# A fp32 decoder layer on one core: where the first norm takes its gain from, who adds the weight sums, and the order of attention's transposes

## The chip, the cores and the metric

The kernel runs on one core of one Trainium2 chip. The metric is the device time of one execution in microseconds (us), the median of several executions. TensorE (PE) multiplies matrices, its weight loads (PEld) run beside it, VectorE (DVE), ScalarE (ACT) and GpSimd (POOL) work element by element, and SyncE (SP) issues the DMAs.

## What is computed

One decoder layer in fp32 with three residual steps, for 16 meta tokens and 1024 tokens of width 1024: a half-step SwiGLU (d_ff 2816), a mix of eight stick-breaking attention heads and eight RWKV-7 heads, and a second half-step SwiGLU; then a last norm without the meta tokens. Cut to the core (the heads' inner functions are left out):

```python
h = jnp.concatenate([meta, x], axis=1)
for l in range(DEPTH):
    n = rms_norm(h, ffn1_norm[l])
    h = h + 0.5 * swiglu(n, ffn1_w_gate[l], ffn1_w_up[l], ffn1_w_down[l])
    n = rms_norm(h, mix_norm[l])
    proj = n @ w_in[l]
    q, k, v = ...                      # 8 heads of 64
    sb_out = stick_breaking_attention(q, k, v)
    rw_out = rwkv7_time_mix(proj[..., 3 * SB_WIDTH:], ...)
    h = h + jnp.concatenate([sb_out, rw_out], axis=-1) @ w_out[l]
    n = rms_norm(h, ffn2_norm[l])
    h = h + 0.5 * swiglu(n, ffn2_w_gate[l], ffn2_w_up[l], ffn2_w_down[l])
return rms_norm(h, final_norm)[:, N_META:]
# A[t,s] = sigmoid(z_ts) * prod_{s<j<t} (1 - sigmoid(z_tj)), o_t = sum_{s<t} A[t,s] v_s
```

## The kernel before

**Arithmetic.** Every fp32 operand is split in two: `split` (L473) lets ACT copy it to a rounded high part and DVE (or POOL, where it is told so) subtract that from the source for the low part. `mm3` (L638) then issues three matmuls for one product: high by high, low by high, high by low. A weight tile arrives by an SP DMA in `wraw` (two buffers), and `wsplit` (L501) makes `whi` (ACT) and `wlo` (DVE) of it.

**Stages.** The tokens go in two groups, A with 528 and B with 512. TensorE's order is FFN1 of A (0 to some 400 us), the projections and part of RWKV of A, FFN1 of B (from 586 us) with RWKV units and A's attention (918 to 1049) strewn in, projections of B, w_out of A, FFN2 of A (from 1323) with RWKV and attention of B (1555 to 1782), w_out of B, FFN2 of B (the last part from 2020 to 2245 in quads) and the last norm.

**Order.** A planner (class `Clock`) runs the kernel's generators as tasks with priorities, holds its own costs for each operation, and emits the one whose data and buffers (`need`) are due; what it emits is the order on each engine. So a moved operation can reorder its neighbours.

**Start.** `xfirst` (L2092) spreads the first norm's gain over the partitions by two matmuls (tile `pg1` in the code, `pg` in the trace), DVE copies them to `g1b`; `block` (L816) multiplies the two first token blocks by `g1b`, scales them by the root (`xn`), transposes them (`pxn`) and splits them to `nh`, `nl`. `raw` (L2128) transposes the raw tokens (`px`) for the residual `h`.

**Quads.** For d_ff tiles from 6 on in FFN1 of A, and at the end of FFN2 of B, gate and up products of two tiles are made with seven half products instead of eight. `pair` (L550) makes the weight sums s1 to s4 (tiles `qs`) on POOL and splits each to `qh`, `ql`; the `quad` generator (L1071) multiplies. There are 30 such pairs. `ups2` (L924) splits the result to `ah` (ACT) and `al` (POOL).

**FFN1 of B.** `ffn` (L851) has `mm`, `gate`, `up`, `down`. The first two d_ff tiles are made for tokens 0 to 256 and then for 256 to 512, and their weights are loaded and split anew for each. `load_n1` (L2308) fetches the normed tokens of B (`nh`, `nl` from the scratch tensor `nbd`) on SP. Beside it, RWKV's `prep` makes the tiles `x` on DVE, for the products `pG`.

**Attention.** `attn_av` (L1815): `trs` transposes one group of weights (`pat`) of the first head, then of the second; the value products (`po`) of the group before follow once its splits (`ath`, `atl`) are done.

**End.** `final_last` (L1992) transposes the last scaled rows (`po`), then adds up the sums of squares (`fss`, twelve and four passes) for the root `fst`; DVE and ACT scale the output `ot`, SP stores it.

Every instruction goes through one recorder, so all rows name line L101: the tiles tell them apart.

Of the kernel before, what the change touches and what calls it, by code (L numbers as in the profile page):

```python
# [16 lines left out]
P = 128  # L17
# [434 lines left out]
class Ker:  # L452
# [48 lines left out]
    def wsplit(self, raw, nk, nm, pool):  # L501
        self.clock.ahead = True
        hi = pool.tile([P, nk, nm], F32R, tag="wh", bufs=2, name="whi")
        lo = pool.tile([P, nk, nm], F32R, tag="wl", bufs=2, name="wlo")
        self.split(hi, lo, raw)
        self.clock.ahead = False
        return hi, lo
# [42 lines left out]
    def pair(self, raws, out):  # L550
# [7 lines left out]
        def part(src=None):  # L558
# [8 lines left out]
            if src:  # L567
                x, y, op = src
                raw = p.tile([P, 4, P], F32, tag="qs", bufs=3, name="qs")
                self.hold((raw,))  # L570
                nc.gpsimd.tensor_tensor(out=raw, in0=x, in1=y, op=op)
# [16 lines left out]
        s1 = yield from part((a2[:, lo4], a2[:, hi4], ALU.add))  # L588
# [5 lines left out]
        s2 = yield from part((s1[1], a1[:, lo4], ALU.subtract))  # L594
# [4 lines left out]
        s4 = yield from part((a1[:, hi4], s2[1], ALU.subtract))  # L599
        halves(*s2)  # L600
        out.append((a22, a22))
        s3 = yield from part((a1[:, lo4], a2[:, lo4], ALU.subtract))
# [213 lines left out]
    def block(self, xts, m, xp, bank, out, hot=None):  # L816
# [10 lines left out]
        with level():  # L827
            for j, (xt, xn) in enumerate(zip(xts, xns)):
                nc.scalar.activation(hot[j] if hot else xn, xt, AF.Square, accum_out=st[:, 0, j:j + 1])
                if hot:  # L830
                    nc.vector.tensor_tensor(out=xn, in0=xt, in1=self.g1b, op=ALU.mult)
            nc.vector.tensor_scalar(out=st[:, 1], in0=st[:, 0], scalar1=1.0 / D, scalar2=RMS_EPS, op0=ALU.mult, op1=ALU.add)
            self.rsqrt(nc.vector, st[:, 2], st[:, 1], st[:, 3])
            for j, (xt, xn) in enumerate(zip(xts, xns)):
# [16 lines left out]
    def ffn(self, nm, h, n, chunks, edge, bank, first=None, hook=None, wx=False, poll=None, resid=None, done=None, wy=False, fast=False):  # L851
# [124 lines left out]
        for part in PARTS:  # L976
# [3 lines left out]
            if f0 == 0 and first:  # L980
# [17 lines left out]
            else:  # L998
                for f in range(f0, f1):
# [204 lines left out]
    def plan(self):  # L1204
# [13 lines left out]
        def ffn(nm, poll=False, wx=False, fast=False):  # L1218
# [7 lines left out]
            for f0, f1 in PARTS:  # L1226
                if fast and f0 >= QF:
                    break
                if f0 == 0:
# [29 lines left out]
        yield from ffn("ffn1")  # L1259
# [555 lines left out]
    def attn_av(self, hp, pr, g, bufs, ops, att):  # L1815
# [611 lines left out]
```

## Time and profile before

| what | us |
|---|---|
| median of 3 executions | 2285.75 (2285.22 to 2285.99) |
| the profiled execution | 2287.36 |
| its span | 2285.4 |
| PE busy | 2242.8 |
| DVE busy | 1563.0 |
| ACT busy | 1093.9 |
| POOL busy | 704.6 |

The profiled execution lies 1.6 us above the median, and 2.0 us of it lie outside the span. Read it in this order: the busy shares, then the chain of waits that ended last, then at the few places where PE stands still what it waited for and what the releaser did before that. A granted clock (PEclk) of 1.00 is 2.4 GHz, 0.50 is 1.2 GHz.

### The profile page before, as it was taken

The numbers are of one execution on the slowest core, as the hardware profiler recorded it, in microseconds if no ns is written. First come the engines' busy times: TensorE is split into PE (matmuls) and PEld (weight loads), VectorE is DVE, ScalarE is ACT, GpSimd is POOL, SyncE is SP. The second block draws the span as 40 slices with busy tenths as digits, with TensorE's granted clock in tenths as the row PEclk, the third lists the DMA queues.
The fourth block names the chain that finished last, engine by engine and source line by source line (L and its number), as shares of the span: only waits on it lengthen the run. The fifth ranks groups of instructions, "written<-read, shape, count | busy, mean of one in ns | idle before, by whom it ended". The sixth has DMA issues, their size and how long they took to land.

```text
span 2285.4 us, 41628 instructions
## 1 busy us (share of the span) xinstructions
PE 2242.8 (98%) x16351; PEld 1982.2 (87%) x16351; DVE 1563.0 (68%) x2593; ACT 1093.9 (48%) x2162; POOL 704.6 (31%) x786
## 2 busy tenths in 40 slices
PE   8999999999999999999999999999999999999998
PEld 7999999999878888778788988787777998898998
DVE  6788776575766655676476878547777565788774
ACT  5444444444444434654434555445665345344444
POOL 1254541013133231541012415325444011255540
PEclk9999999999999999999999989999999999999999
DMA  4643242545743233332546534333222533333332
GB/s 131 203 112 100 85 112 74 162 132 138 223 116 98 75 101 96 100 88 72 174 138 183 149 82 123 85 94 105 86 75 70 158 93 120 93 102 111 102 93 74
DMA packets 411546, 258.64 MB, mean 113 GB/s; under 512 B 45006, under 2 KB 396454, under 8 KB 411351
## 3 DMA queue, kind: packets, MB, share of 16 engines
q1 hardware_dynamic: 411350, 256.00, 38.7%
q8 instruction: 128, 2.10, 0.4%
q14 instruction: 68, 0.55, 0.1%
HBM read 221.95 MB, written 33.99 MB: 112 GB/s over the span
## 4 chain that ended last, share of the span: by engine, by line
PE 87%; DVE 6%; DMA 2%; ACT 2%; issue 1%; SPq 1%; POOL 0%; DVEq 0%; ACTq 0%; POOLq 0%
PE pd L101 33%; PE pu L101 20%; PE pg L101 19%; PE px L101 3%; PE pwo L101 3%; PE po L101 2%; PE pz L101 2%; DVE wlo L101 2%; PE pat L101 2%; DVE ql L101 1%; SPq L101 1%; ACT whi L101 1%; PE pG L101 1%; DMA wraw<-in_ffn_w_down_dram 1%; DMA wraw<-in_ffn_w_up_dram 1%
## 5 line engine op out<-in xcount | busy, mean ns | idle before, releaser
L101 ACT ACTIVATE whi<-wraw 128x1024 fp32r<-128x1024 f32 (+1 forms) x318 | 334.8, 1053 | 331.3 <-PE pd L101 196.8
L101 DVE TENSOR_TENSOR wlo<-wraw,whi 128x1024 fp32r<-128x1024 f32 (+1 forms) x318 | 423.2, 1331 | 94.2 <-ACT whi L101 86.7
L101 PE MATMUL pd<-ah,whi 128*128 128x512 f32 (+2 forms) x944 | 327.3, 347 | 2.6 <-DVE h L101 1.6
L101 PE MATMUL pd<-ah,wlo 128*128 128x512 f32 (+2 forms) x944 | 319.1, 338 | 0.0
L101 PE MATMUL pd<-al,whi 128*128 128x512 f32 (+2 forms) x944 | 318.5, 337 | 0.6 <-DVE al L101 0.5
L101 PE MATMUL pd<-nh,whi 128*128 128x256 f32 (+7 forms) x648 | 210.4, 325 | 0.0
L101 PE MATMUL pu<-nh,whi 128*128 128x512 f32 (+3 forms) x584 | 210.0, 360 | 0.0
L101 PE MATMUL pd<-nl,whi 128*128 128x256 f32 (+7 forms) x648 | 204.5, 316 | 0.0
L101 PE MATMUL pd<-nh,wlo 128*128 128x256 f32 (+7 forms) x648 | 204.4, 315 | 0.0
L101 PE MATMUL pu<-nh,wlo 128*128 128x512 f32 (+3 forms) x584 | 201.0, 344 | 0.7 <-DVE wlo L101 0.7
L101 PEld LDWEIGHTS pd<-ah,whi 128*128 128x128 f32 x944 | 177.7, 188 | 27.4 <-issue 5.0
L101 PE MATMUL pu<-nl,whi 128*128 128x512 f32 (+3 forms) x584 | 200.9, 344 | 0.0
L101 PE MATMUL pg<-nh,whi 128*128 128x512 f32 (+3 forms) x544 | 200.7, 369 | 0.0
L101 POOL TENSOR_TENSOR al<-sl,ah 128x512 fp32r<-128x512 f32 (+2 forms) x47 | 77.6, 1651 | 391.2 <-ACT ah L101 327.9
L101 PEld LDWEIGHTS pd<-ah,wlo 128*128 128x128 f32 x944 | 177.6, 188 | 20.4
L101 PEld LDWEIGHTS pd<-al,whi 128*128 128x128 f32 x944 | 177.8, 188 | 18.4 <-DVE al L101 1.4
L101 PE MATMUL pg<-nl,whi 128*128 128x512 f32 (+3 forms) x544 | 190.9, 351 | 0.1
L101 PE MATMUL pg<-nh,wlo 128*128 128x512 f32 (+3 forms) x544 | 190.7, 351 | 0.3 <-DVE wlo L101 0.3
L101 DVE SCALAR_TENSOR_TENSOR h<-pd,h 128x256 f32<-128x256 f32 (+1 forms) x200 | 107.4, 542 | 74.6 <-PE pd L101 73.6
L101 PEld LDWEIGHTS pd<-nh,whi 128*128 128x128 f32 (+2 forms) x648 | 120.1, 185 | 12.5 <-issue 3.1
L101 PEld LDWEIGHTS pd<-nh,wlo 128*128 128x128 f32 (+2 forms) x648 | 120.1, 185 | 8.6
L101 POOL TENSOR_TENSOR qs<-wraw 128x512 f32<-128x512 f32 x60 | 92.9, 1548 | 111.5 <-DVE ql L101 41.1
(390 smaller groups left out, 5779.9 us busy)
## 6 DMA issues: line engine op xcount, KB each, us to landing
wraw<-in_ffn_w_gate_dram SPq DMA_DIRECT2D x92, 512.0 KB
wraw<-in_ffn_w_up_dram SPq DMA_DIRECT2D x92, 512.0 KB
wraw<-in_ffn_w_down_dram SPq DMA_DIRECT2D x88, 512.0 KB
wraw<-in_w_in_dram SPq DMA_DIRECT2D x54, 512.0 KB
wraw<-in_w_out_dram SPq DMA_DIRECT2D x18, 512.0 KB
s<-rkvd SPq DMA_DIRECT2D x18, 256.0 KB
raw<-qkvd SPq DMA_DIRECT2D x16, 264.0 KB
raw<-qkvd SPq DMA_DIRECT2D x16, 256.0 KB
```

The costliest lines, as they stand in the source:

```text
L101: self._c.trace(self._n, op, lambda: f(*a, **k), out, [x for x in args if isinstance(x, bass.AP)], k)
```

## The change

1. **Start.** DVE multiplies the two first blocks by the gain straight from PSUM, in four pieces of 512; `g1b` is copied by ACT behind that. The low parts of the first two weight tiles go to POOL. The raw transposes of the two first blocks (16 `px`) go ahead of the normed ones.
2. **Quads.** Sums s2 and s4 of all 30 pairs and the 28 wide `al` of `ups2` go from POOL to DVE.
3. **Half a norm is enough.** `mm` asks for the first four k tiles, then for the others.
4. **FFN1 of B, `once`.** Only d_ff tile 0 goes by ranges, with its weights kept for both; tile 1 goes in whole 512. Four weight loads and splits fewer; 96 matmuls of 256 columns become 48 of 512. The loads of `load_n1` are urgent, so they go ahead of weights on SP.
5. **Attention.** Transposes of both heads go together, behind the splits of the group before, and that group's value products directly after them.
6. **End.** The last 256 columns are scaled by DVE to a tile `hs` while ACT squares them; all sums but the last stand ahead of the last transposes.

```diff
+        self.nsplit = getattr(self, "nsplit", 0) + 1
         hi = pool.tile([P, nk, nm], F32R, tag="wh", bufs=2, name="whi")
         lo = pool.tile([P, nk, nm], F32R, tag="wl", bufs=2, name="wlo")
-        self.split(hi, lo, raw)
+        self.split(hi, lo, raw, self.nc.gpsimd if self.nsplit < 3 else None)
...
-                x, y, op = src
+                x, y, op, eng = src
                 raw = p.tile([P, 4, P], F32, tag="qs", bufs=3, name="qs")
                 self.hold((raw,))
-                nc.gpsimd.tensor_tensor(out=raw, in0=x, in1=y, op=op)
+                eng.tensor_tensor(out=raw, in0=x, in1=y, op=op)
...
-        s1 = yield from part((a2[:, lo4], a2[:, hi4], ALU.add))
+        s1 = yield from part((a2[:, lo4], a2[:, hi4], ALU.add, nc.gpsimd))
...
-        s2 = yield from part((s1[1], a1[:, lo4], ALU.subtract))
+        s2 = yield from part((s1[1], a1[:, lo4], ALU.subtract, nc.vector))
...
-        s4 = yield from part((a1[:, hi4], s2[1], ALU.subtract))
+        s4 = yield from part((a1[:, hi4], s2[1], ALU.subtract, nc.vector))
...
-        s3 = yield from part((a1[:, lo4], a2[:, lo4], ALU.subtract))
+        s3 = yield from part((a1[:, lo4], a2[:, lo4], ALU.subtract, nc.gpsimd))
...
-                if hot:
-                    nc.vector.tensor_tensor(out=xn, in0=xt, in1=self.g1b, op=ALU.mult)
+                for q in range(2 if hot else 0):
+                    qs = slice(512 * q, 512 * q + 512)
+                    nc.vector.tensor_tensor(out=xn[:, qs], in0=xt[:, qs], in1=self.g1p[q], op=ALU.mult)
...
+            if hot:
+                self.flags["xn"] = True
...
-            yield self.need(*[x[k][:, c0:c1] for k in range(KT) for x in n[0:2]], bank=self.nextbank)
+            yield self.need(*[x[k][:, c0:c1] for k in range(4) for x in n[0:2]], bank=self.nextbank)
             ps = bank(name)[:, :c1 - c0]
             for k in range(KT):
+                if k == 4:
+                    yield self.need(*[x[k][:, c0:c1] for k in range(4, KT) for x in n[0:2]])
...
-                    self.split(a[0][:, 0:2 * self.fast.w], a[1][:, 0:2 * self.fast.w], x, nc.gpsimd)
+                    self.split(a[0][:, 0:2 * self.fast.w], a[1][:, 0:2 * self.fast.w], x)
...
+                if f0 == 0 and once:
+                    wg = yield from gu(gw, 0, True)
+                    act.append(act_tiles())
+                    for i, c in enumerate(edge):
+                        yield from first(i)
+                        sl = yield from gate(wg, *c)
+                        if i:
+                            self.drop(wg)
+                        else:
+                            wu = yield from gu(uw, 0, True)
+                        yield from up(wu, sl, act[0], *c, False)
+                        self.drop((sl,))
+                    self.drop(wu)
+                for f in range(f0 + (f0 == 0 and once), f1):
...
-            hs = []
-            for h in range(2):
-                yield self.need(*[a[h] for a in att], bank=(psa, "t", bufs["t"]))
-                yield from self.room(ap, ("ath", bufs["at"]), ("atl", bufs["at"]))
-                hs.append(tr(grp, h))
-            return grp, hs
+            for t in ("ath", "atl"):
+                yield self.two(bank=(ap, t, bufs["at"]))
+            yield self.two(*[x for a in att for x in a], bank=(psa, "t", bufs["t"]))
+            return grp, [tr(grp, h) for h in range(2)]
         prev = yield from trs(grps[0])
         for grp in grps[1:] + [None]:
+            yield self.need(*[x for hs in prev[1] for x in hs[0:2]])
             nxt = (yield from trs(grp)) if grp else None
             if grp is grps[-1]:
                 for x in att:
                     self.drop(x)
-            yield self.need(*[x for hs in prev[1] for x in hs[0:2]])
             av(*prev)
...
+            if m == KT - 1:
+                sums = self.norm_sums(s(), 256, "fss", bank)
+                for _ in s()["last"]:
+                    yield next(sums)
+                last = next(sums)
+                src = s()["scaled"]
+            else:
+                src = h2[:, m, cs]
+            yield self.need(src)
...
-                nc.tensor.transpose(out=pts[m // 4 * 2 + b][:, m % 4 * P:m % 4 * P + P], in_=h2[:, m, cs.start + b * P:cs.start + b * P + P],
+                nc.tensor.transpose(out=pts[m // 4 * 2 + b][:, m % 4 * P:m % 4 * P + P], in_=src[:, b * P:b * P + P],
                                     identity=self.ident)
-        st, _ = yield from self.norm_sums(s(), 256, "fss", bank)
+        yield last
+        st, _ = yield from sums
...
+            self.g1p = []
             for q in range(2):
                 yield self.need(g1r, bank=self.tbank)
                 ps = tb("pg1")
+                self.g1p.append(ps)
+                self.hold((ps,))
                 nc.tensor.matmul(ps, lhsT=self.ones[0:1, :], rhs=g1r[:, 512 * q:512 * q + 512], start=True, stop=True)
-                with self.urgent():
-                    nc.vector.tensor_copy(out=self.g1b[:, 512 * q:512 * q + 512], in_=ps)
             F["g1b"] = True
+            yield lambda: F.get("xn")
+            for q, ps in enumerate(self.g1p):
+                nc.scalar.activation(self.g1b[:, 512 * q:512 * q + 512], ps, AF.Copy)
+            self.drop(self.g1p)
...
+            for j in range(2):
+                ck.spawn(raw(xs[j], *blks[j], h, True), 32)
...
+                    if (i, m, late[i]) == (1, KT - 1, 3):
+                        y = fp.tile([P, 512], F32, tag="sl", bufs=2, name="hs")[:, 0:256]
+                        with self.urgent():
+                            nc.vector.tensor_scalar(out=y, in0=x, scalar1=self.v(gain, m), scalar2=None, op0=ALU.mult)
+                        ssq[key, i]["scaled"] = y
+                    else:
+                        nc.scalar.activation(x, x, AF.Copy, scale=self.v(gain, m))
...
-                        nc.sync.dma_start(out=n[2 + j][q][:, :, cs].bitcast(F32), in_=self.nbd[j, :, 4 * q:4 * q + 4, cs])
+                        with self.urgent():
+                            nc.sync.dma_start(out=n[2 + j][q][:, :, cs].bitcast(F32), in_=self.nbd[j, :, 4 * q:4 * q + 4, cs])
...
-            yield from self.ffn("ffn1", h, n, ch, chB, bank, lambda i: (), hookB)
+            yield from self.ffn("ffn1", h, n, ch, chB, bank, lambda i: (), hookB, once=True)
```

**At the start**, ScalarE before (`xq` squares a block, `whi` is a weight's high part, `pxn` the transposed normed tokens, `px` the raw ones):

```order
L101 ACTIVATE g1w<-ones 128x1
L101 ACTIVATE xq,bst<-xt 128x1024 x2
L101 ACTIVATE whi<-wraw 128x1024 x2
L101 ACTIVATE nh_147<-pxn 128x4x128
L101 ACTIVATE nh_148<-pxn 128x4x128
```

and now:

```order
L101 ACTIVATE g1w<-ones 128x1
L101 ACTIVATE g1b<-pg_177 128x512
L101 ACTIVATE xq,bst<-xt 128x1024
L101 ACTIVATE g1b<-pg_179 128x512
L101 ACTIVATE h<-px 128x4x128
L101 ACTIVATE xq,bst<-xt 128x1024
L101 ACTIVATE h<-px 128x4x128 x3
L101 ACTIVATE whi<-wraw 128x1024 x2
L101 ACTIVATE nh_147<-pxn 128x4x128
L101 ACTIVATE nh_148<-pxn 128x4x128
```

Two copies of the gain and four copies of raw tokens now stand ahead of the first split on ScalarE; on PE the 16 raw transposes stand between the gain's two matmuls and the 16 normed transposes.

**At the entry to FFN1 of B**, SP's queue before (`nbd` holds the normed tokens of B; 147 and 149 are the high and low parts of k tiles 0 to 3, 148 and 150 of 4 to 7):

```order
L101 DMA nh_148<-nbd 128x4x256
L101 DMA wraw<-in_ffn_w_gate_dram 128x8x128
L101 DMA qkvd_3_86<-qst 128x272
L101 DMA nl_150<-nbd 128x4x256
L101 DMA wraw<-in_ffn_w_up_dram 128x8x128
L101 DMA qkvd_7_90<-qst 128x272
L101 DMA wraw<-in_ffn_w_gate_dram 128x8x128
L101 DMA nh_147<-nbd 128x4x256
```

and now:

```order
L101 DMA nh_148<-nbd 128x4x256
L101 DMA nl_150<-nbd 128x4x256
L101 DMA qkvd_3_86<-qst 128x272
L101 DMA wraw<-in_ffn_w_gate_dram 128x8x128
L101 DMA wraw<-in_ffn_w_up_dram 128x8x128
L101 DMA qkvd_7_90<-qst 128x272
L101 DMA nh_147<-nbd 128x4x256
L101 DMA nl_149<-nbd 128x4x256
```

The first gate weight now stands behind the last normed tokens of the first range and a store of projections; the normed tokens of the second range stand ahead of the next weight.

**In a quad of FFN2 of B**, POOL before:

```order
L101 TENSOR_TENSOR al<-cc,ah 128x512 x2
L101 TENSOR_TENSOR qs<-wraw 128x512
L101 TENSOR_TENSOR qs<-qs,wraw 128x512
L101 TENSOR_TENSOR qs<-wraw,qs 128x512
L101 TENSOR_TENSOR qs<-wraw 128x512
```

and VectorE now, in the last quad (`ql` is a low part of a sum, `cc` the quad's combinations, `pg` and `pu` its products):

```order
L101 TENSOR_TENSOR al<-cc,ah 128x512
L101 TENSOR_TENSOR wlo<-wraw,whi 128x1024
L101 TENSOR_TENSOR ql<-wraw,qh 128x512
L101 TENSOR_TENSOR cc<-pg,sn 128x256
L101 TENSOR_TENSOR qs<-qs,wraw 128x512
L101 TENSOR_TENSOR ql<-qs,qh 128x512
L101 TENSOR_TENSOR cc<-pg,sn 128x256 x2
L101 TENSOR_TENSOR cc<-cc,sg 128x512 x2
L101 SCALAR_TENSOR_TENSOR h2B<-pd,h2B 128x512
L101 TENSOR_TENSOR qs<-wraw,qs 128x512
L101 TENSOR_TENSOR ql<-qs,qh 128x512
```

The second and the fourth sum and both `al` of a pair moved into VectorE's row, between its other subtractions; the first and third sum stay on POOL.

## Rows read from the trace of the kernel before

**Rows 1.** The page: busy time by engine, and the chain that ended last

```profile
PE 2242.8 (98%) x16351; PEld 1982.2 (87%) x16351; DVE 1563.0 (68%) x2593; ACT 1093.9 (48%) x2162; POOL 704.6 (31%) x786
...
PE 87%; DVE 6%; DMA 2%; ACT 2%; issue 1%; SPq 1%; POOL 0%; DVEq 0%; ACTq 0%; POOLq 0%
```

**Rows 2.** Timeline, start: start us, duration, engine, operation, count, idle before

```profile
6.16 0.69 DVE L101 COPY g1b<-pg 128x512 f32<-128x512 f32 x1 [1.01 <-PE pg L101]
...
6.89 2.36 DVE L101 TENSOR_TENSOR xn<-xt,g1b 128x1024 f32<-128x1024 f32 x2
6.95 1.06 ACT L101 ACTIVATE xq<-xt 128x1024 f32<-128x1024 f32 x1 [0.15 <-DMA xt<-in_x_dram]
...
10.62 1.23 DVE L101 TENSOR_TENSOR wlo<-wraw,whi 128x1024 fp32r<-128x1024 f32 x1
...
12.57 3.67 PE L101 MATMUL pxn<-ident,xn 128*128 128x128 f32 x16 [6.44 <-DVE xn L101]
...
16.80 0.53 PE L101 MATMUL pg<-nl,whi 128*128 128x256 f32 x1
```

**Rows 3.** Timeline of PE alone, raw transposes among the first gate products

```profile
23.71 1.04 PE L101 MATMUL px<-ident,xt 128*128 128x128 f32 x8
24.50 0.36 PE L101 MATMUL pg<-nh,whi 128*128 128x256 f32 x1
```

**Rows 4.** Groups by form, whole span: count, busy, mean ns, idle before

```profile
L101 DVE TENSOR_TENSOR ql<-qs,qh 128x512 fp32r<-128x512 f32 x120 | 120.5, 1025 | 2.4 <-ACT qh L101 2.3
...
L101 POOL TENSOR_TENSOR qs<-wraw,qs 128x512 f32<-128x512 f32 x30 | 54.3, 1810 | 3.6 <-DVE ql L101 1.4
```

**Rows 5.** Timeline, first quads of FFN2 of B

```profile
2045.88 0.68 DVE L101 TENSOR_TENSOR ql<-qs,qh 128x512 fp32r<-128x512 f32 x1
...
2047.42 1.45 DVE L101 TENSOR_TENSOR ql<-qs,qh 128x512 fp32r<-128x512 f32 x1
...
2048.93 0.39 PE L101 MATMUL pu<-t2h,ql 128*128 128x256 f32 x1 [0.62 <-DVE ql L101]
```

**Rows 6.** PE's waits, whole span: waited for, us in total, times, longest

```profile
PE pu L101 <- DVE ql L101: 3.4, 8, 0.8
PE pG L101 <- DVE x L101: 2.4, 1, 2.4
...
PE pg L101 <- DVE ql L101: 2.2, 2, 1.6
```

**Rows 7.** Windows: stretch, length, busy (count) by engine, PEclk, DMA share, GB/s

```profile
600.80:607.70 6.90, 6.00 (x33) 5.78 (x34) 6.58 (x11) 0.66 (x1) 0.16 (x1) 0.51 0.45 142
905.00:1050.00 145.00, 145.00 (x803) 114.48 (x802) 96.14 (x144) 80.93 (x182) 62.12 (x77) 1.00 0.33 96
2080.00:2160.00 80.00, 80.00 (x538) 73.68 (x538) 63.62 (x77) 37.81 (x65) 42.48 (x26) 1.00 0.36 101
1327.90:1341.50 13.60, 13.37 (x89) 13.08 (x89) 8.91 (x22) 5.46 (x15) 0.00 (x0) 0.50 0.28 78
```

**Rows 8.** Timeline, entry to FFN1 of B

```profile
599.98 1.66 DVE L101 TENSOR_TENSOR x<-pe,s 64x640 f32<-64x640 f32 x1
```

**Rows 9.** Timeline of PE, attention of A: a transpose pair between gate products

```profile
931.71 0.39 PE L101 MATMUL pat<-ident,sg 128*16 128x128 f32 x2
931.85 0.48 PE L101 MATMUL pg<-nh,whi 128*128 128x512 f32 x1
932.17 0.40 PE L101 MATMUL pg<-nl,whi 128*128 128x512 f32 x1
932.41 0.39 PE L101 MATMUL pg<-nh,wlo 128*128 128x512 f32 x1
```

**Rows 10.** Timeline, the end

```profile
2275.35 0.51 ACT L101 ACTIVATE h2B<-h2B,vec 128x256 f32<-128x256 f32 x1
...
2275.91 0.44 PE L101 MATMUL po<-ident,h2B 128*128 128x128 f32 x2 [1.29 <-ACT h2B L101]
...
2276.55 1.48 PE L101 MATMUL fss<-ones,nsq 128*128 128x1 f32 x12
```

More of the change, by code (lines that the diff above doesn't have):

```diff
@@ L848, in block, with ffn @@
             self.drop((xn,))
-    def ffn(self, nm, h, n, chunks, edge, bank, first=None, hook=None, wx=False, poll=None, resid=None, done=None, wy=False, fast=False):
+    def ffn(self, nm, h, n, chunks, edge, bank, first=None, hook=None, wx=False, poll=None, resid=None, done=None, wy=False, fast=False, once=False):
         nc, A, tp = self.nc, self.A, self.fp
@@ L979, in ffn @@
                 break
-            if f0 == 0 and first:
+            if f0 == 0 and first and not once:
                 get, have = kept(lambda i, keep: gu((gw, uw)[i % 2], i // 2, keep))
@@ L998, in ffn @@
             else:
-                for f in range(f0, f1):
+                if f0 == 0 and once:
[12 more added lines that the diff above has]
+                for f in range(f0 + (f0 == 0 and once), f1):
                     if f > f0 or f == 0:
@@ L1216, in wout, with ffn @@
                 yield cols("w_out", m * P, P)
-        def ffn(nm, poll=False, wx=False, fast=False):
+        def ffn(nm, poll=False, wx=False, fast=False, once=False):
             gu = lambda c, f: cols(nm + "_w_" + c, f * P, P)
@@ L1228, in ffn @@
                     break
-                if f0 == 0:
+                if f0 == 0 and once:
+                    yield from [gu(c, f) for f in range(f0, f1) for c in ("gate", "up")]
+                elif f0 == 0:
                     yield from kept([gu(c, f) for f in range(f0, f1) for c in ("gate", "up")])
@@ L1258, in plan @@
         yield from proj(0)
-        yield from ffn("ffn1")
+        yield from ffn("ffn1", once=True)
         yield from proj(1)
@@ L1997, in final_last @@
             yield lambda: s()["k"] > min(max(m, m // 4 * 6), KT - 1)
-            yield self.need(h2[:, m, cs])
+            if m == KT - 1:
[7 more added lines that the diff above has]
+            yield self.need(src)
             for b in range(2):
@@ L2120, in startup @@
             yield lambda: F.get(("blk", 4))
-            for xt, (t0, m) in zip(xs, blks):
+            for xt, (t0, m) in zip(xs[2:], blks[2:]):
                 yield from raw(xt, t0, m, h)
@@ L2126, in startup, with raw @@
                 ck.spawn(groupB(j), 11 - j)
-        def raw(xt, t0, m, h):
+        def raw(xt, t0, m, h, hot=False):
             for q in range(2):
-                yield self.need(xt, bank=self.tbank)
-                pt = tb("px").rearrange("p (k t) -> p k t", t=P)[:, :, 0:m]
+                yield self.need(xt, bank=self.nextbank if hot else self.tbank)
+                pt = (self.bank if hot else tb)("px").rearrange("p (k t) -> p k t", t=P)[:, :, 0:m]
                 for k in range(4):
@@ L2161, in hook @@
                     x = hh[:, m, slice(*ch[i])]
-                    nc.scalar.activation(x, x, AF.Copy, scale=self.v(gain, m))
+                    if (i, m, late[i]) == (1, KT - 1, 3):
[5 more added lines that the diff above has]
+                        nc.scalar.activation(x, x, AF.Copy, scale=self.v(gain, m))
                 return ssq[key, i]["k"] == KT
```

## The prediction

> **What bounds the kernel now.** I read the busy shares first: TensorE works 2242.8 us of a span of 2285.4, VectorE 1563 and the others half or less, and the chain that ended last is 87% TensorE [rows 1]. So two kinds of gain exist: fewer or shorter PE instructions, and the 43 us in which PE stands still. The list of PE's waits shows where [rows 6]: for VectorE's low parts in the quads (3.4 + 2.2 us) and once 2.4 us before the RWKV product `pG`. The rest is mostly the start, up to the first gate products at 16.80 us [rows 2], and the end, after 2274 us [rows 10]. Third come stretches at the lower granted clock: 600.8 to 607.7 and 1327.9 to 1341.5 at 0.5, that is 1.2 GHz, each with little or no PE idle of its own [rows 7]. Where PE is full, 145.00 of 145 in A's attention, 80.00 of 80 in steady quads [rows 7], a faster VectorE brings nothing, and a slower one costs only when it becomes the last.
>
> **Start: -2.2 us.** Before, the second gain copy ends at 6.85, two multiplications take 2.36, the root's small operations end at 10.62, a weight subtraction of 1.23 is pushed in, and the scaled block is ready for PE at 12.57 [rows 2]. The subtraction goes to POOL. The gain copies go to ScalarE, with four `h` copies of the same size; VectorE took 0.69 for such a copy [rows 2], and I take 0.6 to 0.7. The second square, at 6.95 and 1.06 long [rows 2], then stands behind two gain copies and one `h` copy, about 1.3 us later, and ends near 9.4. The root needs it; its operations (from 6.89 + 2.36 = 9.25 to 10.62, 1.4) end near 10.9, and scaling lets the transposes start 0.7 after that, near 11.7 instead of 12.57. From the transposes to the first low-part product it was 16.80 - 12.57 = 4.2, so 15.9 on this path. The other path is ScalarE: behind the square three more `h` copies and two weight copies (1.9 + 2.1) hold its first `nh` until 13.4; three `nh` of 0.6 and a subtraction of 0.7 make 15.9 as well. With two queues meeting I take 16.2: 0.6 gained, from -0.5 (a still later square) to 1. Second, 16 raw transposes leave the full stretch after 23 us: eight cost 24.50 - 23.71 = 0.79 [rows 3], so 16 cost 1.6, and PE idles anyway where they go, before 12.57. At the lower clock they take twice as long, 3.2 us, and still end before 11.8. Together -2.2, bounds 0 and -3.
>
> The Trainium skill, PSUM — Partial Sum Buffer, Terms, says that two engines that touch one bank and quadrant at once collide, reads against reads included. This speaks against reading the gain by DVE and ScalarE from one bank. No row of before has the pair; if the two queues alternate as it asks, that is the 0.6 of a gain copy in the second square's delay, and the start would be about -2.8 without it.
>
> **Quads: -2 us.** A pair moves two sums to VectorE and nearly one `al` each (28 over 30 pairs): 2.93 operations. Alone, such a subtraction of 128x512 takes 0.68, next to a POOL operation 1.45 [rows 5], on the mean of 120 1.025 [rows 4]; POOL needs 1.8 for one [rows 4]. What VectorE gains: 2.93 x 0.68 = 2.0 us a pair. What it loses: the 120 `ql` are 0.345 each above 0.68, 41 us, that is 1.4 a pair, at 3.93 POOL operations a pair, so 0.35 for each of the 2.93 that leave, 1.0 a pair, and more if `wlo` and `cc` stretch likewise. The balance is 0 to +1 us a pair. VectorE has 63.62 of 80 us in steady quads [rows 7], 0.80 of the time, some 12 us where a pair has 15 (15 pairs in the 225 us from 2020 to 2245); it stays under PE. What gets shorter is the chain: the second and the fourth sum, each made from the one before, took POOL 1.8 each [rows 4] and take VectorE 0.7 to 1.5. This matters only in the first quads of each batch, where pairs run back to back and PE waits: 0.62 for `ql` in one row [rows 5], 5.6 in all [rows 6]. I take a third of that, -2; the bounds are -5.6 and +6 (the same waits twice).
>
> The Trainium skill, SBUF — State Buffer, Who interferes with whom, says that a DVE instruction with two SBUF inputs contends with a GpSimd instruction that reads SBUF, and the loser blocks for the whole of the other. The 0.68 and 1.45 agree. By that rule the moved sums, which have two SBUF inputs, are themselves open to blocking by the POOL sums that stay; that is rival A.
>
> **FFN1 of B: -4.8 us.** PE waits 2.4 us for RWKV's `x` [rows 6], whose last part takes 1.66 on VectorE, slowed beside POOL [rows 8]; right behind it stand 6.9 us at clock 0.51 [rows 7], in which half the work is lost, about 3.4 us. After the change the products in front of `pG` are a longer run: by the order of PE, 42 matmuls of 256 columns stand between the last recurrence and `pG`, 27 before; a product of 512 columns takes 932.41 - 932.17 = 0.24 [rows 9], so one of 256 some 0.12, and that is 5.0 us in place of 3.2. With `sl` moved between the parts of `x`, the wait goes down by 1.8 at least; and as the weights come half as often, four splits (about 1.06 of ScalarE and 1.23 of VectorE [rows 2]) go from this stretch, which gives the rest. So -2.4 for the wait, -3.4 for the clock, if the pause alone brought it down. Merging 96 products of 256 columns into 48 of 512 is worth next to nothing, 0.2: both stream the same columns. Against it stand the urgent loads: on SP the first gate weight now stands behind the last normed tokens and a store. I bound this new wait by nothing and by the 2.4 of the wait that goes [rows 6], and take half. Sum -2.4 - 3.4 - 0.2 + 1.2 = -4.8; bounds 0 (wait and clock as before, elsewhere) and -8 (no new wait, and the weights' own delays in this stretch gone too).
>
> **Attention: 0.** The planner pays for each switch between transposes and products; the trace does not. From two transposes through one product to the next product is 931.71 to 932.17, 0.46 [rows 9], and two transposes at 0.79 / 8 [rows 3] and one product at 0.24 are 0.44. So fewer switches save at most 0.02 a piece, 1 us for the 46 fewer that the order of PE shows. On the other side the transposes now stand behind the splits of the group before. PE is full there [rows 7] because FFN products fill in, and the planner still has them. Bounds -2 and +5.
>
> **The half norm** in `mm`: nothing outside the start, since PE is full elsewhere and asks for norms long done.
>
> **End: -1.7.** The last scaling ends on ScalarE, and PE waits 1.29 for it; then two transposes from 2275.91 and sixteen sums of 0.12, the last twelve 1.48 [rows 10]. After the change VectorE scales while ScalarE squares, so transposes start about the 0.51 of the scaling earlier, say 0.45, and four sums in place of sixteen follow: 12 x 0.12 = 1.4. Of that 1.85 I leave 0.15 for DVE's place in line. Bounds -1 and -1.9; nothing in the profile can hide this, as the output hangs on it.
>
> **Untouched stretches.** Between 1050 and 1550 the order of all engines is the same, so no term; but the lower clock at 1327.9 [rows 7] may move with phase: about 6 us of PE work are lost there. I allow 3 us either way.
>
> Sum: -2.2 - 2 - 4.8 + 0 - 1.7 = -10.7. The profiled execution, 2287.36, would become 2276.7; it stands 1.6 above the median, so the median 2285.75 becomes **2275.1 us**.
>
> **Rivals.** *A, VectorE becomes the bound in quads (slower).* If the sums are blocked on VectorE as `ql` is at 2047.42, 0.77 each, 2.93 of them make +2.3 on top of the +1 above, and VectorE's 12 us a pair become 15.3: above the pair's 15. Then PE waits in all 30 pairs as it waits in the first ones, about 0.9 each: 27 - 5.6 = +21, less the other terms' 8.7: 2298. For it speaks 0.80 share [rows 7] and the 0.68-to-1.45 rows; against it, that fewer POOL operations are there to block. It decides from VectorE over 98% of a steady quad stretch. *B, the entry keeps its price.* The gate weight comes late, PE pauses there in place of at 601, and the clock drops all the same: that term is 0, and the time 2279.9 with quads, 2281.9 without them. The late weight in SP's order speaks for it; that the new pause, as I price it, is half the one before the drop speaks against it. *C, attention's new wait shows.* Transposes behind the splits cost a quarter to a half of the 0.62 that PE waits for a subtraction in the quads [rows 5] in each of 72 groups, 11 to 22 us; at the lower end 2275.1 + 12 = 2287. PE's 145.00 of 145 speaks against. *D, the middle's dip also goes,* as everything shifts by some us: 2275.1 - 6 = 2269.
>
> **How the numbers follow.** Forecast 0.58 (2275.1, from 2269 to 2281), D 0.14, B 0.16, C 0.05, A 0.07. The bounds of the terms, taken together, reach about 8 us to either side, and the range takes in D, B and the lower part of C: 2264 to 2287; A is left out. Differences of 0.2%, 4.6 us, are about what a measurement of this kernel can tell from none. Faster than 2281.2: forecast, D and near half of B, 0.79; the other half of B with C: 0.14; A: 0.07.
>
> **What would show it.** Right: the first gate product's `nl` near 16.1 and no `px` of eight in the stream at 23 us; `ql` waits under 4 us in sum, the mean `ql` near 0.9; no wait over 1.5 us at `pG` and clock 1.00 from 595 to 610; attention windows still full; the root `fst` about 1.7 earlier before the end. Wrong: VectorE above 95% in 2080 to 2160 (A), a clock of 0.5 near 590 to 610 (B), many waits `pat` for `ath` or `atl` (C). The forecast falls altogether if a new pause in the reordered stretches, 586 to 830 or the attention, brings the clock down once more.

## The result

| kernel | median, us | lowest to highest | runs |
|---|---|---|---|
| before | 2285.87 | 2285.22 to 2286.32 | 4 |
| after | 2272.34 | 2267.69 to 2274.84 | 4 |

The changed kernel takes 0.9939 of the time of before, with an interval of 0.9921 to 0.9956: 13.5 us less, where 10.7 were forecast. The time lies in the range and the sign is right. The working behind it is right in part only, as the next table shows: one term came to nothing and another to nearly four times its size.

The profile of after is of an execution of 2273.33 us. Its page, busy time and chain, against [rows 1]:

```profile
PE 2239.5 (99%) x16303; PEld 1979.7 (87%) x16303; DVE 1566.0 (69%) x2673; ACT 1085.4 (48%) x2157; POOL 555.8 (24%) x700
...
PE 94%; DVE 2%; ACT 1%; DMA 1%; issue 1%; SPq 0%; POOL 0%; DVEq 0%; ACTq 0%; POOLq 0%
```

TensorE's share of the chain rose from 87% to 94%, VectorE's fell from 6% to 2%; POOL lost 149 us of work, and VectorE, which took it over, is busy only 3 us longer.

**Where the time went.** I took the same PE instruction in both traces (the first `nps` of FFN1 of A, the last `pwo`, and so on) and subtracted its start. The change of that offset over a stretch is what the stretch gained:

| stretch, us of before | forecast | measured |
|---|---|---|
| start, to 141 | -2.2 | -3.25 |
| quads, FFN1 of A and FFN2 of B | -2 | -3.4 and -4.2 |
| projections of A, 400 to 566 | 0 | +0.4 |
| FFN1 of B, 566 to 1088 | -4.8 | -0.1 |
| attention of B, 1590 to 1908 | 0 | +0.8 |
| same order, 1088 to 1590 | 0 (3 either way) | -2.6 |
| end | -1.7 | -1.55 |

**Start.** Timeline of after, where the columns are those of [rows 2]:

```profile
5.21 0.69 DVE L101 TENSOR_TENSOR xn<-xt,pg 128x512 f32<-128x512 f32 x1 [5.21 <-DMA xt<-in_x_dram]
...
5.99 3.67 PE L101 MATMUL px<-ident,xt 128*128 128x128 f32 x16
...
6.81 0.60 ACT L101 ACTIVATE g1b<-pg 128x512 f32<-128x512 f32 x1 [0.49 <-DVE xn L101]
...
7.78 1.06 ACT L101 ACTIVATE xq<-xt 128x1024 f32<-128x1024 f32 x1
...
11.35 1.97 PE L101 MATMUL pxn<-ident,xn 128*128 128x128 f32 x16 [1.69 <-DVE xn L101]
...
14.74 0.39 PE L101 MATMUL pg<-nl,whi 128*128 128x256 f32 x1 [0.56 <-DVE nl L101]
```

The first low-part product starts at 14.74 where 16.2 was forecast: the second square is 0.83 later than before and not 1.3, and the 16 normed transposes take 1.97 in place of 3.67 [rows 2]. The sign of no `px` of eight near 23 us did not come: sixteen fewer follow in the stream, but the third block's first eight now stand at 24.10.

**Entry to FFN1 of B.** Timeline of after, the pause of PE and what ScalarE did ahead of it; then the window behind the pause (columns as in [rows 7]):

```profile
580.21 1.06 ACT L101 ACTIVATE whi<-wraw 128x1024 fp32r<-128x1024 f32 x1
...
581.29 0.27 ACT L101 ACTIVATE rsv<-pu 64x128 f32<-64x128 f32 x1
...
581.60 0.28 DVE L101 COPY rsv<-pu 64x128 f32<-64x128 f32 x1 [1.02 <-ACT rsv L101]
...
581.94 1.10 PE L101 MATMUL px<-rsv,bg 128*128 128x64 f32 x8 [1.64 <-DVE rsv L101]
```

```profile
583.40:593.60 10.20, 10.20 (x49) 9.95 (x48) 4.60 (x11) 2.90 (x10) 1.25 (x2) 0.51 0.75 225
...
595.00:610.00 15.00, 15.00 (x119) 13.52 (x118) 11.33 (x22) 3.53 (x6) 2.84 (x5) 1.00 0.22 61
```

The wait at `pG` is gone and the clock stands at 1.00 from 595 to 610, as forecast. But the first gate weight comes later, so no gate products lie between two RWKV steps; PE waits 1.64 for a copy of `rsv`, which on ScalarE stands behind a weight copy of 1.06. Behind that wait come 10.2 us at half clock (a granted clock of 0.5), in place of 6.9 [rows 7].

**Quads.** Groups by form of after, against [rows 4]:

```profile
L101 DVE TENSOR_TENSOR ql<-qs,qh 128x512 fp32r<-128x512 f32 x120 | 90.6, 776 | 0.0
L101 DVE TENSOR_TENSOR qs<-wraw,qs 128x512 f32<-128x512 f32 x30 | 33.6, 1118 | 0.0
```

The mean `ql` fell from 1025 to 776 ns: 30 us in 120 of them, which pays for more than a third of the 88 operations that VectorE took over; its other operations on SBUF shrink as well, and four weight subtractions are gone. Of the ten waits for `ql` of before [rows 6] one is left, 1.0 us.

**End.** Timeline of after, against [rows 10]:

```profile
2262.48 0.35 DVE L101 TENSOR_SCALAR hs<-h2B,vec 128x256 f32<-128x256 f32 x1
...
2263.30 0.41 PE L101 MATMUL po<-ident,hs 128*128 128x128 f32 x2
...
2263.55 0.51 PE L101 MATMUL fss<-ones,nsq 128*128 128x1 f32 x4
2264.09 0.16 DVE L101 TENSOR_SCALAR fst<-fss 128x2 f32<-128x2 f32 x1 [1.26 <-PE fss L101]
```

Four sums of squares follow the last transposes in place of sixteen.

### The profile page after: what moved, and what is told of

Its sections match the earlier page's. It is cut to its first block, busy times and chain, and to the rows that moved or that the text cites. A ratio compares the mean times of both kernels' runs of the same rounds, so it can differ in the third digit from the quotient of the medians.

```text
span 2271.4 us, 41476 instructions
## 1 busy us (share of the span) xinstructions
PE 2239.5 (99%) x16303; PEld 1979.7 (87%) x16303; DVE 1566.0 (69%) x2673; ACT 1085.4 (48%) x2157; POOL 555.8 (24%) x700
## 4 chain that ended last, share of the span: by engine, by line
PE 94%; DVE 2%; ACT 1%; DMA 1%; issue 1%; SPq 0%; POOL 0%; DVEq 0%; ACTq 0%; POOLq 0%
PE pd L101 34%; PE pu L101 22%; PE pg L101 21%; PE pwo L101 4%; PE px L101 3%; PE po L101 2%; PE pz L101 2%; PE pat L101 2%; PE pG L101 1%; DVE wlo L101 1%; PE psw L101 0%; DMA wraw<-in_ffn_w_gate_dram 0%; SPq L101 0%; PE pp L101 0%; ACT whi L101 0%
## 5 line engine op out<-in xcount | busy, mean ns | idle before, releaser
L101 ACT ACTIVATE whi<-wraw 128x1024 fp32r<-128x1024 f32 x314 | 330.6, 1053 | 333.9 <-PE pd L101 208.8
L101 DVE TENSOR_TENSOR wlo<-wraw,whi 128x1024 fp32r<-128x1024 f32 (+1 forms) x312 | 401.0, 1287 | 88.6 <-ACT whi L101 83.8
L101 POOL TENSOR_TENSOR qs<-wraw 128x512 f32<-128x512 f32 x60 | 101.5, 1697 | 359.3 <-DVE ql L101 142.3
```

Of the source, the lines that this page charges most:

```text
L101: self._c.trace(self._n, op, lambda: f(*a, **k), out, [x for x in args if isinstance(x, bass.AP)], k)
```

## The experiments

All edits are to the kernel after, and ratios are to the kernel before, run on the same chip. Executions of most of these kernels scatter by 4 to 9 us, as stretches of half clock come and go, so a part is read from the offsets in the trace, which repeat to 0.1 us where order and clock are the same. Each kernel has one trace, of one execution.

**1. The changed kernel once more.** No edit.

> The changed kernel once more, to see what its own executions do. Theory: after the change TensorE pauses 1.6 us near 580 us and the granted clock then falls to 0.5 for about 10 us, which costs some 5 us, in some executions and not in others; so times lie in two clusters, near 2267.5 and near 2272 to 2275, median 2271 to 2273. Rival: the lower clock stands there every time and the spread comes from other places; then times scatter evenly over 2268 to 2275.

2273.7 us (2269.13 to 2277.45), ratio 0.9955 [0.9941, 0.9968]. Offsets: start -3.02, quads -3.39 and -4.17, FFN1 of B +0.2; 10.2 us at half clock again from 584.4. The rival holds so far: the drop at the entry is there in all nine traces with this entry, for 6.8 to 13.7 us. That length and other places make the scatter; the executions without a trace can't be told apart.

**2. The quads' work back on POOL.**

```diff
-        s2 = yield from part((s1[1], a1[:, lo4], ALU.subtract, nc.vector))
+        s2 = yield from part((s1[1], a1[:, lo4], ALU.subtract, nc.gpsimd))
...
-                    self.split(a[0][:, 0:2 * self.fast.w], a[1][:, 0:2 * self.fast.w], x)
+                    self.split(a[0][:, 0:2 * self.fast.w], a[1][:, 0:2 * self.fast.w], x, nc.gpsimd)
```

(s4 like s2.)

> The changed kernel with the sums s2 and s4 and the wide low parts al back on GpSimd; TensorE's order is the same. Theory: the offsets between the two traces (-3.4 us over the first quads, -4.2 over the last) are due to this part alone; so 7.6 us come back, 2279 to 2281, the mean ql is near 1.02 us again and TensorE waits 7 to 9 us for ql. Rival, the prediction's term: it is worth 2 us, 2274 to 2275, and the rest of the offsets came from elsewhere.

2280.85 us, ratio 0.9986 [0.9977, 0.9995]; quads -0.03 and -0.02 in place of -3.39 and -4.17. The mean `ql` is 1023 ns again, and PE waits 5.5 us for `ql`, as in before and under the 7 to 9 expected. The whole of the 7.6 us is this part; the median, 7.2 above that of experiment 1 on the same chip, agrees.

**3. All four sums on VectorE.** In `quad`, s1 and s3 with `nc.vector` in place of `nc.gpsimd`.

> The changed kernel with all four sums on VectorE, none on GpSimd; TensorE's order is the same. Theory: in the quads VectorE loses about as much to GpSimd as the moved work costs, so two sums more a pair leave its share of 2080 to 2160 between 0.80 and 0.88 and the time within 2 us of the changed kernel's, 2270 to 2274, with ql near 0.69 us. Rival A of the prediction: VectorE is already close to the bound, its share goes over 0.95, TensorE waits for ql in steady quads, and the time is 2280 or more.

2269.42 us (2268.59 to 2277.88), just under the range expected, ratio 0.9936 [0.9921, 0.9952]; quads -2.84 and -4.42. First the groups, then the window of steady quads, of this kernel; then the same window of after:

```profile
L101 DVE TENSOR_TENSOR ql<-qs,qh 128x512 fp32r<-128x512 f32 x120 | 81.6, 682 | 0.6 <-ACT qh L101 0.3
...
L101 DVE TENSOR_TENSOR qs<-wraw,qs 128x512 f32<-128x512 f32 x30 | 20.5, 682 | 0.0
```

```profile
2080.00:2160.00 80.00, 80.00 (x551) 74.33 (x550) 63.23 (x102) 38.91 (x66) 0.00 (x0) 1.00 0.41 112
```

```profile
2080.00:2160.00 80.00, 80.00 (x551) 74.27 (x550) 66.94 (x94) 38.26 (x67) 17.27 (x11) 1.00 0.37 106
```

With POOL idle such an operation takes 682 ns on the mean, and VectorE, with 25 operations more than in before [rows 7], is busy 63.23 of 80 us against 63.62. Rival A falls: what VectorE takes over, it gets back from the stretching that ends. The Trainium skill, SBUF — State Buffer, Who interferes with whom, has a VectorE operation with two SBUF inputs and a GpSimd operation that reads SBUF lock each other out; 682 alone, 776 with some POOL work and 1025 with more agree.

**4. Sums back on POOL, `al` on VectorE.** The s2 line of experiment 2, and s4.

> The changed kernel with only the sums s2 and s4 back on GpSimd (al stays on VectorE); TensorE's order is the same. Theory: TensorE waits in the first quads for the chain of sums on GpSimd, so 6 to 7.6 us come back, 2278 to 2281. Rival: the gain goes by the number of GpSimd operations that left (two of three), 4.5 to 5.5 us, 2277 to 2279.

2273.75 us, ratio 0.9940 [0.9921, 0.9958]; quads -0.14 in FFN1 of A and -4.02 in FFN2 of B. The ratio is that of after, so the median doesn't show the 3.4 us of the trace.

**5. `al` back on POOL, sums on VectorE.** The second line pair of experiment 2.

> The changed kernel with only al back on GpSimd (the sums stay on VectorE); TensorE's order is the same. Theory: al stands after the products of a pair and delays no sum in the first quads by more than a GpSimd operation, so 0 to 1.5 us come back, 2272 to 2275. Rival, by the number of operations that left: 2 to 3 us, 2274.5 to 2276.

2275.51 us, ratio 0.9952 [0.9936, 0.9968]; quads -3.30 and -1.63. The timeline of this kernel's PE shows the wait that came back in FFN2 of B:

```profile
2053.42 0.38 PE L101 MATMUL pg<-t2h,ql 128*128 128x256 f32 x1 [2.10 <-DVE ql L101]
```

Behind this wait stand 3.4 us at half clock (2054.85 to 2058.26), so not all of what is lost there is the wait.

Experiments 4 and 5 together, by the traces: in FFN1 of A the sums are worth 3.25 of the 3.39. In FFN2 of B moving the `al` back costs 2.5 of the 4.2 with the half clock in it, and with `al` on VectorE the sums can stay on POOL. Neither expectation held for both places.

**6. The raw transposes back in the stream.**

```diff
-            for j in range(2):
-                ck.spawn(raw(xs[j], *blks[j], h, True), 32)
...
-            for xt, (t0, m) in zip(xs[2:], blks[2:]):
+            for xt, (t0, m) in zip(xs, blks):
```

> The changed kernel with the 16 raw transposes of the two first blocks back in the later stream; the gain is still read in PSUM and the first two low parts are still made on GpSimd. Theory: what lets the 16 normed transposes run at full clock from 11.35 us is the work of the raw ones before them; without them they take 3.7 us, not 1.97, the first low-part product comes at 15.3 to 16.8 us instead of 14.74, the 1.6 us return to the stream, and at 141 us the offset to the kernel before is between 0 and -1.2 instead of -3.25; time 2274 to 2276.5. Rival: the clock is up by 11.35 us whatever TensorE did; then 1.97, 14.2 to 14.8, an offset of -1.4 to -1.9, and 2273 to 2275.

2279.59 us (2274.2 to 2282.34), ratio 0.9966 [0.9952, 0.9981]; the offset at 141 us is +1.33 in place of -3.25. PE at the start of this kernel:

```profile
10.91 1.97 PE L101 MATMUL pxn<-ident,xn 128*128 128x128 f32 x8 [4.82 <-DVE xn L101]
13.68 1.97 PE L101 MATMUL pxn<-ident,xn 128*128 128x128 f32 x8 [0.80 <-DVE xn L101]
...
16.21 0.58 PE L101 MATMUL pg<-nl,whi 128*128 128x256 f32 x1
```

Here 8 transposes take the 1.97 that 16 take in after, and the first low-part product comes where the theory had it; the offset and the time do not. Nor is it shown that the raw transposes bring the full rate: in experiment 4 they stand ahead too, and the 16 normed ones take 3.68. Between these two traces the place of the raw transposes is worth 4.6 us, more than the whole gain of the start; 1.6 was forecast for taking them out of the stream. Against experiment 4, whose first products are as slow as here, it is still 3.8 (+1.33 against -2.43), so the rate of the first products is the smaller part. Waits of 0.37 and 0.45 at 118.33 and 119.17, which before has too and neither after nor experiment 4 has, are 0.8 of it. How the rest divides isn't settled.

**7. The loads of the normed tokens not urgent.** In `load_n1`, `if True:` in place of `with self.urgent():`.

> The changed kernel with load_n1's DMAs not urgent, as before, so that the first gate weight goes ahead of the last normed tokens and the recurrence's px products again stand behind gate products. Theory: the 1.6 us pause near 580 us goes, the clock stays at 1.00 from 580 to 600, and the time is 5 to 7 us below the changed kernel's, 2265 to 2268, in every execution. Rival: the clock falls anyway behind another pause (the RWKV pG products or the late weights), and the time is 2270 to 2274.

2274.38 us, ratio 0.9959 [0.9946, 0.9971]; FFN1 of B +0.3. PE's wait and the window behind it, of this kernel:

```profile
596.66 2.02 PE L101 MATMUL pG<-x,bk 64*128 64x128 f32 x14 [2.37 <-DVE x L101]
```

```profile
596.60:603.50 6.90, 5.81 (x32) 5.55 (x33) 4.30 (x11) 0.63 (x1) 0.00 (x0) 0.51 0.06 19
```

The pause moves back to `pG`, where before has it [rows 6, 7], and the clock falls there. The urgent loads trade one pause for another, and a drop comes with either. The merged tile alone does not shorten the wait: 21 products stand between the recurrence and `pG` here, 27 in before and 42 in after.

**8. One `rsv` copy on VectorE.** The fourth chunk's copy in the first RWKV unit of B:

```diff
-                nc.scalar.activation(rsv[R[1], :, c, 1, :], pu[R[1]], AF.Copy)
+                if s["u"] == 0 and s["pr"] == 0 and c == 3:
+                    V.tensor_copy(out=rsv[R[1], :, c, 1, :], in_=pu[R[1]])
+                else:
+                    nc.scalar.activation(rsv[R[1], :, c, 1, :], pu[R[1]], AF.Copy)
```

> The changed kernel, where the one ScalarE copy of rsv in the fourth chunk of the first RWKV unit, which stands behind a weight copy of 1.06 us, is made by VectorE. Theory: the pause at 580 us goes down from 1.64 to about 0.6 to 1.1 us and the granted clock stays at 1.00 from 580 to 600; it saves some 0.8 + 5 us, and the time is 2266 to 2269. Rival: the lower clock follows that pause too, or the one at pG comes back, and the time is 2271 to 2275.

2264.48 us (2262.4 to 2268.07), ratio 0.9904 [0.9889, 0.9919]; FFN1 of B -7.5. The same place in this kernel:

```profile
582.22 1.21 PE L101 MATMUL px<-rsv,bg 128*128 128x64 f32 x8 [0.53 <-DVE rsv L101]
```

```profile
580.00:600.00 20.00, 19.21 (x163) 18.35 (x162) 13.82 (x30) 8.73 (x21) 2.11 (x3) 1.00 0.63 188
```

One copy of 0.28 moved from one queue to the other: the pause shrinks from 1.64 to 0.53, a little more than expected, and the clock stays up, as it does in experiment 12, the other trace with this copy. Of the 7.5 us, 1.1 are the pause and some 5 the half clock of 10.2 us that doesn't follow; the rest was not traced further.

**9. FFN1 of B as before.** Without `once=True`, and the loads as in experiment 7.

> The changed kernel with FFN1 of B as before: two d_ff tiles by ranges, weights loaded anew, the normed tokens not urgent. Theory: the change of this stretch moved the pause and the low clock from pG to the px products and gained 0.1 us net; so the wait of 2.4 us at pG and the clock of 0.5 behind it return, the wait at px goes, and the offset over 566 to 1088 changes by less than 1.5 us; time 2271 to 2276. Rival, the prediction's term: 4.8 us slower, 2277 to 2278.

2277.54 us (2273.26 to 2280.92), ratio 0.9972 [0.9961, 0.9984]. PE's waits in this kernel, and the windows behind them:

```profile
596.77 2.08 PE L101 MATMUL pG<-x,bk 64*128 64x128 f32 x14 [2.38 <-DVE x L101]
...
609.37 1.87 PE L101 MATMUL pG<-x,bk 64*128 64x128 f32 x14 [1.55 <-ACT gate L101]
```

```profile
596.00:602.80 6.80, 6.03 (x33) 5.80 (x34) 6.45 (x11) 1.00 (x1) 0.04 (x1) 0.50 0.43 136
609.60:613.00 3.40, 3.40 (x22) 3.18 (x21) 2.67 (x6) 0.67 (x1) 0.00 (x0) 0.51 0.44 120
```

FFN1 of B takes 6.2 us longer than in before itself with nearly the same order there: the wait for `gate` grew from the 0.6 of before to 1.55 and has a second drop behind it, and a third came at 855. So against after this trace puts the part at 6.3 us, among them two drops of 3.4 us that before has not, though the stretch itself shows only -0.1 between before and after. The median is 3.8 above that of experiment 1, on the same chip, and lies in the rival's range, not in the theory's; but the pause and the drop at `pG` did come back as the theory had it. The parts don't add here, and why the `gate` wait grew was not traced further.

**10. Attention as before.** `trs` by heads, and the value products' `need` behind the next transposes.

> The changed kernel with attention's transposes by head as before, ahead of the splits of the group before. Theory: the regrouping is worth nothing, since a switch on TensorE costs nothing; the offset between the entry and the end of A's attention stays within 1 us of the changed kernel's, the same for B's, and the time is 2270 to 2275. Rival, the planner's price of 0.085 us for each of 46 switches, or the waits behind the splits that the change adds: 4 us slower or faster, with its place in the attention stretches.

2271.44 us (2268.62 to 2275.07), ratio 0.9946 [0.9928, 0.9963]. Offsets over attention of A and of B: 0 and 0, where after has +0.55 and +0.78. PE's waits from 1555 to 1790, of this kernel and then of after:

```profile
PE pat L101 <- DVE atl L101: 1.2, 1, 1.2
PE pg L101 <- DVE wlo L101: 0.3, 1, 0.3
```

```profile
PE pd L101 <- DVE wlo L101: 1.2, 2, 0.9
```

The regrouping removes a wait for a split (`atl`) and gets one for weights (`wlo`). It gains nothing and costs about 1.3 us of trace, which the median can't resolve. The waits don't explain the cost: in B they sum to 1.45 here and 1.20 in after. What does was not traced further.

**11. The end as before.** The last rows scaled on ScalarE, the sums behind the transposes.

> The changed kernel with the old end: the last columns scaled on ScalarE, all sums after the last transposes; all else the same. Theory: 1.6 us later from the last h2B to fst, and 1 to 2 us in the time, 2272 to 2275. Rival: the order of the end is hidden by the store, no change in the distance from the last product to the end.

2275.04 us (2273.04 to 2276.98), ratio 0.9967 [0.9954, 0.998]. The end of this kernel:

```profile
2264.34 0.51 ACT L101 ACTIVATE h2B<-h2B,vec 128x256 f32<-128x256 f32 x1
...
2264.90 0.44 PE L101 MATMUL po<-ident,h2B 128*128 128x128 f32 x2 [1.29 <-ACT h2B L101]
...
2265.54 1.48 PE L101 MATMUL fss<-ones,nsq 128*128 128x1 f32 x12
2267.05 0.16 DVE L101 TENSOR_SCALAR fst<-fss 128x2 f32<-128x2 f32 x1 [3.20 <-PE fss L101]
```

From the last addition (at 2263.43, in after at 2262.02) to `fst` it takes 3.62 us, in after 2.07: 1.55 us are the end's. The median, 1.3 above that of experiment 1, can't resolve it.

**12. Experiments 8 and 10 in one kernel.**

> Both earlier findings in one kernel: the fourth copy of rsv of the first RWKV unit of B on VectorE, and attention in its old form. Theory, the two add up: the stretch 565 to 1088 gains some 7 us as with the copy alone, and attention takes 0.5 less in 918 to 1088 and 0.8 less in 1590 to 1888 than in the changed kernel; against the kernel before 2263 to 2265 us, ratio near 0.990. Rival, the 1.3 of attention was phase and not form: the time stays where the copy alone put it, and other small waits or a dip of the clock of 3.4 us or more appear in their place in 918 to 1088 or 1590 to 1888.

2263.06 us (2259.13 to 2265.34), ratio 0.9906 [0.9889, 0.9922]. FFN1 of B with attention of A gains 7.7, 0.3 more than with the copy alone where 0.5 was expected, and attention of B stands at 0 instead of +0.8, so in the trace the two nearly add up. The median is 1.4 under that of experiment 8, inside their scatter. The trace is of the fastest execution, with 3.4 us of half clock near 1314. Both versions are faster than before and after; that the second edit helps is shown by the trace alone.

## Why the prediction was right in sum and wrong in two terms

**Start (-2.2, measured -3.25): right in kind, a little outside its bound of -3, its two parts sized wrong.** The path to the first product gained 2.06 where 0.6 was forecast, mostly because the normed transposes ran at twice the rate, which the working did not consider. That rate is luck of the execution (see the last section), and it shows less at 141 us: in experiments 1 and 10 the transposes took 3.31 and 2.57, and the offset there is -3.02 and -1.97; over all traces with this start it is -1.94 to -3.25. The steadier part is the raw transposes' place, 3.8 to 4.6 in experiment 6 where 1.6 was forecast. On the bank that two engines read, no rows of after have both at once: ScalarE's second copy, 0.60 from 6.81, stands between the two of VectorE's pieces that read the same half of the gain (6.09 to 6.78, and from 7.77). The collision that the Trainium skill (PSUM — Partial Sum Buffer, Terms) warns of was neither shown nor refuted.

**Quads (-2, measured -7.6): right cause, size wrong, outside its bound.** The failed step is "I take a third of that". Nearly all the waits went, and experiment 2 brings them back. And the 5.6 is itself too little: it holds only idle time that the list puts on `ql`. PE's busy time shows the same two stretches of the first quads in before, and then in after:

```profile
100.00:260.00 160.00, 157.38 (x1278) 155.75 (x1277) 136.77 (x195) 78.85 (x145) 90.17 (x59) 1.00 0.35 99
...
2015.00:2140.00 125.00, 121.25 (x893) 114.69 (x893) 107.19 (x127) 62.82 (x114) 73.40 (x44) 1.00 0.34 96
```

```profile
100.00:260.00 160.00, 160.00 (x1317) 160.00 (x1317) 136.92 (x216) 78.31 (x140) 41.02 (x26) 1.00 0.35 100
...
2015.00:2140.00 125.00, 123.98 (x903) 117.35 (x902) 106.94 (x154) 63.47 (x114) 28.97 (x17) 1.00 0.36 102
```

2.6 and 2.7 us of idle went, 5.35 together, and some 2.2 more in the first products behind each pause: the wait of 0.62 [rows 5] moved all that follows by 0.78. The mean `ql` was forecast near 0.9 and came to 0.776; VectorE's share of a steady stretch rose from 0.80 to 0.84, far from rival A's 0.98. (The working counts 3.93 POOL operations a pair; four sums and 28 `al` over 30 pairs make 4.93, so what VectorE loses to each is 0.28 and not 0.35. The term doesn't rest on it.)

**FFN1 of B (-4.8, measured -0.1): wrong; rival B happened.** "I bound this new wait by nothing and by the 2.4 of the wait that goes, and take half" gave 1.2, and the wait is 1.64; so the price of the wait was near. What failed is the -3.4 for the clock: it rested on the new pause being too short to bring the clock down. The clock fell for 10.2 us, some 5 us lost, which with the 1.64 outweighs the 5.8 that was to go; and of that the 3.4 was a little much, as the half clock of before begins at 600.84, 0.9 us ahead of the end of its pause. The prediction's last line says that the forecast falls altogether if a new pause here brings the clock down. It did, and the time held for another reason, the quads. The working also looked for the wait in the wrong queue: at SP's late weight, and not at what the late weight uncovers, ScalarE's weight copy ahead of `rsv`. Experiment 8 shows that: with that one copy elsewhere the stretch gains 7.5. The wait at `pG` went, but not by the merged tile alone: with the loads as before (experiment 7) it is 2.37 again. Whether the urgent loads alone would remove it, no run shows.

**Attention (0, measured +0.55 and +0.78): right within its bounds.** Rival C's wait behind the splits does not show; PE stays at 145.00 of 145 from 905 to 1050.

**The same order (0, measured -2.6): luck within the allowance.** Before has a second drop of 3.4 us at 1355 that after has not; rival D's drop near 1321 stayed, 13.7 us long. The allowance of 3 either way was itself too small: over the traces of the twelve experiments this stretch reads from +0.9 (experiment 3) to -7.9 (experiment 6).

**End (-1.7, measured -1.55): right,** in both halves (experiment 11).

The sum was near because the quads' missing 5.6 and the start's 1 stood against FFN1 of B's 4.7 too much, and the 2.6 of the same order about covers the rest. That these came so near to each other is luck.

## What to carry to other kernels

Price a new pause of the matrix engine by what the clock does behind it, and look at everything on the releasing engine's queue, not only at the queue that was changed: here one copy of 0.28 us, moved out from behind a weight copy of 1.06, gained 7.5 us. Where VectorE and GpSimd share elementwise work on SBUF, VectorE may take over GpSimd's part for next to nothing, as it did here, since its own operations shrink; but ask place by place which of the moved operations the matrix engine waits for. Of waits that a change removes outright, count all, and a little more than their idle time. And take the same stretch of several traces before reading a gain from one: here a stretch that no edit touched moved by up to 7.9 us.

## What the runs showed of the hardware that I had not expected

**Pauses and the clock.** Half clock follows some pauses of PE and not others of the same length. In the fourteen traces, between 20 and 2250 us and by the listed idle time, the 1.64 at the entry was followed by it in all nine traces that have it, for 6.8, 10.2 or 13.7 us, and the five pauses of 2.10 to 2.38 each had it, for 3.4 or 6.8 (in some of these it begins before the pause ends). Of the eight others from 1.38 to 1.82, three were followed by it, for 3.4 each (1.38, 1.55 and 1.77), and five were not, among them the 1.57 for `ql` in before [rows 6] and one of 1.82 at 1218.70 in experiment 8. A pause of 0.98, found in all of them between 515 and 522, stands ahead of a drop of 3.4 us in experiments 4, 6, 7 and 9 and not in the other ten traces, and near 1321 a drop comes in all fourteen with pauses of 0.7 to 1.2. So the length of a pause alone doesn't decide it. The same pause is followed by different lengths in different runs: the drop near 1321, with the same order around it, lasted 13.7 us in after, 10.2 in experiment 1 and 3.4 in experiments 8 and 12.

**The start.** With the raw transposes ahead, the 16 normed ones took 1.97 us in after and in experiments 2, 5, 7 and 12, 2.57 in 8 and 10, and 3.31 to 3.68 in 1, 3, 4, 9 and 11, from the same code. Apart from the two products for the gain, only transposes came before them. The durations go with the granted clock. Its first record in a trace, of 1.00, begins at 9.65 to 10.26 us in the five traces with 1.97 and at 14.33 to 17.37 in the five with 3.31 to 3.68 (at 17.16 in before, at 17.80 in experiment 6). In experiments 8 and 10 it begins at 9.2, and 0.50 follows from 12.65 to 19.48. Ahead of its first record the clock column shows 1.00 for want of a record, so there the rate is read from the durations. Two windows of after, then one of experiment 8:

```profile
6.00:11.20 5.20, 3.66 (x17) 3.26 (x16) 3.93 (x12) 4.71 (x10) 0.00 (x0) 1.00 1.09 346
11.20:14.00 2.80, 2.17 (x17) 1.92 (x17) 1.96 (x4) 2.80 (x6) 2.58 (x1) 1.00 0.26 97
```

```profile
12.70:19.40 6.70, 6.33 (x29) 5.76 (x28) 4.18 (x13) 3.94 (x8) 3.89 (x2) 0.50 0.50 147
```

In after the 16 raw transposes fill the first window at 0.23 each, the 16 normed ones the second at 0.12. So with one and the same start the full clock came at times that lie up to 8 us apart; what decides between them, no run here shows.
